# A two-layer encoder: layer 1's attention turned by DMA instead of TensorE, with its steps spread further apart

## The chip, the cores and the metric

The kernel runs on one core of a Trainium2 chip. The metric is the time of one execution on the device, in microseconds (us); the times given are medians of several runs. The core has five engines, each with an instruction queue of its own that it works through strictly in order: TensorE (PE, with PEld for its weight loads), VectorE (DVE), ScalarE (ACT), GpSimd (POOL) and SyncE (SP). Engines wait for one another through semaphores. DMA transfers are issued from the queues of SP, ACT and POOL.

## The reference

The input is 256 tokens of width 2048 and 256 memory tokens. Two layers follow each other. Layer 0 mixes tokens by a gated MLP over chunks, layer 1 by grouped-query attention; both also cross-attend with four heads into the memory, and each is followed by a SwiGLU feed-forward network. The part that the change touches is the attention of layer 1:

```python
def gqa_axial_attention(qkv, g_q, g_k, cos, sin):
    q, k, v = jnp.split(qkv, [TOK_WIDTH, TOK_WIDTH + KV_WIDTH], axis=-1)   # 12 query heads, 4 key heads of 128
    q = apply_axial_rope(rms_norm(q, g_q), cos, sin)
    k = apply_axial_rope(rms_norm(k, g_k), cos, sin)
    ...
        s = jnp.einsum('bqhgd,bkhd->bhgqk', qi, k).astype(jnp.float32) * scale
        p = jax.nn.softmax(s, axis=-1).astype(v.dtype)
        return jnp.einsum('bhgqk,bkhd->bqhgd', p, v)
```

Everything is in float32.

## The kernel before

**Products in three matmuls.** Each float32 operand is split into a rounded half `hi` (ACT, a cast) and the rest `lo` (DVE, a subtraction); `matmul3` (L186 to L188) adds three products of halves. Weights come by SP's DMA into `raw` (4 buffers) and are split by `halves` into `whi` (L270, ACT) and `wlo` (L271, DVE), three buffers each. In layer 1's mixing each split is done in two instructions of 128x1024.

**Linear layers and ticks.** `linear(parts, w, n0)` makes 512 output columns for both token tiles of 128: 96 matmuls of 128x512 into two PSUM banks `acc`. The pool of `acc` has four banks, so a linear layer can begin only when the results of the one before the last have been read out. After every 12 matmuls comes a `tick()`; `later(n, f)` puts work of another kind n ticks ahead, and so decides where it is recorded between the matmuls. A scheduler then sets the final order of every engine's queue, which is fixed when the kernel is built.

**Layer 1's mixing** runs these linear layers one after the other: own keys, own values, three groups of four query heads (c = 0, 1, 2; here the first, second and third group), memory queries, memory keys, memory values, and then the output projection `w_out` (four linear layers). They are called the first to the eighth layer below, w_out apart; the third to the fifth make the query groups, the sixth the memory queries, the seventh the memory keys, the eighth the memory values.

**A group's attention** (`attend`) has four steps, put at ticks by `waits`: `queries_T` turns the rotary-embedded queries (`turning`, L474 to L481, which read `acc`) so that the head dimension lies on the partitions; `scores` multiplies by the turned keys into a PSUM bank `m` and does the softmax (maximum L557 on DVE, a product on POOL L558, exp L562 on ACT, reciprocal L566 and scaling L568 on DVE, head by head); `turn` turns the probabilities; `weigh` multiplies by the values. The pool `m` has four banks too. Nearly all of these tiles come from one pool of 36 (`big`, `MIX_TILES`); the pool `kept` has 16 of its own. A tile whose pool is full waits until an older one has been used for the last time.

**Two ways to turn a tile.** On TensorE: `transpose4` (L192), or the same four matmuls by the identity in `turn` (L585), 128x128 each, into a bank `m`. By DMA: `turned`, in which an engine sorts the float32 words into two planes of 16 bits (L199), the ACT queue issues a DMA transpose (L200), and after some ticks an engine puts the planes together again (L205), here over the source. Layer 0 and the feed-forward networks turn by DMA already; layer 1's own keys, own queries, their probabilities, and its memory keys and queries are turned by TensorE, the probabilities of its memory attention by DMA.

Of the kernel before, what the change touches and what calls it, by code (L numbers as in the profile page):

```python
# [55 lines left out]
def encoder(ctx: ExitStack, tc: tile.TileContext, x, x_t, mem, mem_t, columns, w_in_a, g_v_a, spatial_t, w_in_b,  # L56
# [33 lines left out]
    def misc():  # L90
        if room["banks"] == 2:
            return banks2()[:, 0]
        return room["m"].tile([P, NB], F32, tag="m", name=nm("m"))
# [13 lines left out]
    def later(delay, fn):  # L107
        queue.append((clock[0] + delay, len(queue), fn))
# [68 lines left out]
    def split(src, shape, home=None):  # L177

        hi, lo = [(home or big)(F32R, shape) for _ in range(2)]
        nc.scalar.copy(hi, src)  # L180
        nc.vector.tensor_tensor(lo, src, hi.bitcast(F32), ALU.subtract)
        return hi, lo

    def matmul3(out, a, b, start, stop):

        nc.tensor.matmul(out, lhsT=a[0], rhs=b[0], start=start, stop=False)  # L186
        nc.tensor.matmul(out, lhsT=a[1], rhs=b[0], start=False, stop=False)  # L187
        nc.tensor.matmul(out, lhsT=a[0], rhs=b[1], start=False, stop=stop)  # L188
# [5 lines left out]
    def turned(src, ticks, then, over=False, copy=nc.scalar.copy, home=None):  # L194


        a, b = [(home or big)(F32, [P, 4, P]) for _ in range(2)]
        planes, back = [i.bitcast(U16).rearrange("p c n -> p (c n)") for i in (a, b)]
        copy(planes.rearrange("p (h n) -> p h n", h=2), src.bitcast(U16).rearrange("p (n h) -> p h n", h=2))  # L199
        nc.scalar.dma_start_transpose(back.rearrange("p (c n) -> p c n", n=P), planes)  # L200

        def finish():
            words = src.rearrange("p (c n) -> p c n", c=4) if over else a
            halves = (src.bitcast(U16) if over else planes).rearrange("p (n h) -> p n h", h=2)
            copy(halves, back.rearrange("p (h n) -> p n h", h=2))  # L205
            then(words)

        later(ticks, finish)
# [275 lines left out]
    def queries(acc, r, gain=None):  # L484

        rh = head_squares(acc, r)
        res = []
        for t in range(NT):
            nc.vector.tensor_scalar(rh[:, 4 * t:4 * t + 4], rh[:, 4 * t:4 * t + 4], r[t], None, ALU.mult)
            if gain is None:  # L490
                res.append(turning(acc[t], rope_t["c"][:, t], rope_t["s"][:, t]))
            else:
                qn = big()
                nc.vector.tensor_tensor(v4(qn), v4(acc[t]), gain.unsqueeze(1).to_broadcast([P, 4, P]), ALU.mult)
                res.append(qn)
        return res, rh
# [17 lines left out]
    def heads_T(qn, dma=False):  # L514

        hi = [big(F32R, [P, 2, S]) for _ in range(2)]
        lo = [big(F32R, [P, 2, S]) for _ in range(2)]

        def halves_of(t, whole):
            ts = slice(t * P, (t + 1) * P)  # L520
            for pr in range(2):
                src = whole[:, 2 * pr:2 * pr + 2, :]
                nc.scalar.copy(hi[pr][:, :, ts], src)
                nc.vector.tensor_tensor(lo[pr][:, :, ts], src, hi[pr][:, :, ts].bitcast(F32), ALU.subtract)

        for t in range(NT):
            if dma:
                turned(qn[t], 3, lambda whole, t=t: halves_of(t, whole), True, nc.vector.tensor_copy)
            else:
                tp = misc()  # L530
                transpose4(qn[t], tp)
                halves_of(t, v4(tp))
        return hi, lo

    def attend(qn, waits, keys, values, kv_of, kc0, parts, dma=None, home=None):


        qn, rows = qn
        by_head = rows.rearrange("p (t h) -> p h t", t=NT)
        st = {}  # L540

        def head(p, h):
            return p[0][h // 2][:, h % 2, :], p[1][h // 2][:, h % 2, :]

        def queries_T():
            st["qT"] = heads_T(qn, dma and home is None)

        def scores(pr):
            for h in (2 * pr, 2 * pr + 1):
                kp_ = head(keys(), kv_of(h))  # L550
                qp_ = head(st["qT"], h)
                sc = misc()
                for t in range(NT):
                    ts = slice(t * P, (t + 1) * P)
                    matmul3(sc[:, t * S:(t + 1) * S], (qp_[0][:, ts], qp_[1][:, ts]), kp_, True, True)
                nmx = small(2)
                nc.vector.tensor_reduce(nmx, sc.rearrange("p (t k) -> p t k", t=NT), AX.X, ALU.max, negate=True)  # L557
                nc.gpsimd.tensor_tensor(nmx, nmx, by_head[:, h], ALU.mult)  # L558
                pe = big()
                sm = small(2)  # L560
                for t in range(NT):
                    nc.scalar.activation(pe[:, t * S:(t + 1) * S], sc[:, t * S:(t + 1) * S], AF.Exp,  # L562
                                         bias=nmx[:, t:t + 1], scale=rows[:, 4 * t + h:4 * t + h + 1],
                                         accum_out=sm[:, t:t + 1])
                rcp = small(2)
                nc.vector.reciprocal(rcp, sm)  # L566
                for t in range(NT):
                    nc.vector.tensor_scalar(pe[:, t * S:(t + 1) * S], pe[:, t * S:(t + 1) * S], rcp[:, t:t + 1], None,  # L568
                                            ALU.mult)
                st["p", h] = pe  # L570

        def turn(pr):
            for h in (2 * pr, 2 * pr + 1):
                pn = st["p", h]
                if dma:
                    def halves_of(whole, h=h):
                        hi, lo = split(whole.rearrange("p (t k) n -> p k t n", t=NT), [P, 2, NT, P], home)
                        st["t", h] = [a.rearrange("p k t n -> p (k t n)") for a in (hi, lo)]

                    turned(pn, 3, halves_of, True, nc.vector.tensor_copy, home)  # L580
                    continue
                pt = misc()
                for t in range(NT):
                    for kc in range(2):
                        nc.tensor.transpose(pt[:, kc * S + t * P:kc * S + (t + 1) * P],  # L585
                                            pn[:, t * S + kc * P:t * S + (kc + 1) * P], ident)
                st["t", h] = split(pt, [P, NB])

        def weigh(pr):
            V = values()  # L590
            po = misc()
            for hh in range(2):
                h = 2 * pr + hh
                kv = kv_of(h)
                phi, plo = st["t", h]
                for kc in range(2):
                    vhi, vlo = V[kc]
                    vs, ks = slice(kv * P, (kv + 1) * P), slice(kc * S, (kc + 1) * S)
                    matmul3(po[:, hh * S:(hh + 1) * S], (vhi[:, vs], vlo[:, vs]), (phi[:, ks], plo[:, ks]),
                            kc == 0, kc == 1)  # L600
            hi, lo = split(po.rearrange("p (h s) -> p h s", h=2), [P, 2, S])
            for hh in range(2):
                for t in range(NT):
                    ts = slice(t * P, (t + 1) * P)
                    parts.put(kc0 + 2 * pr + hh, t, hi[:, hh, ts], lo[:, hh, ts])

        later(waits[0], queries_T)
        for wait, f in zip(waits[1:], (scores, turn, weigh)):
            for pr in range(2):
                later(wait + pr, lambda f=f, pr=pr: f(pr))  # L610
# [14 lines left out]
    class Memory:  # L625
# [38 lines left out]

        def attend(self, acc, r, parts, waits, dma, home=None):
            attend(queries(acc, r, ghead[f"mq{self.l}"]), waits, lambda: self.kT, lambda: self.V, lambda h: h, TOK // P,
                   parts, dma, home)

    def add_residual(acc, j, norm, g, parts, dma, copy=nc.scalar.copy):

# [20 lines left out]
    for l in range(DEPTH):  # L691
# [121 lines left out]
                    later(1 + t, lambda u=u, t=t, c=c: turn_u(u, t, c))  # L813
        else:
            w = w_in_b[0]
            own = {}
            load_tables(1)
            m.prep(20, 2)
            acc = linear(hT, w, TOK)
# [7 lines left out]
                    nc.gpsimd.tensor_tensor(s[:, :, h], s[:, :, h], g4[:, :, 1 - h], ALU.mult)  # L827

            def turn_k(kn=kn):
                own["k"] = heads_T(kn)  # L830

            later(7, turn_k)
            own["v"] = scaled(linear(hT, w, TOK + MEMW), norm.r)
            for c in range(3):
                acc = linear(hT, w, c * NB)
                attend(queries(acc, norm.r), (5, 6, 11, 14), lambda: own["k"], lambda: own["v"],
                       lambda h, c=c: (4 * c + h) // 3, 4 * c, cat)
            m.attend(linear(hT, w, TOK + 2 * MEMW), norm.r, cat, (4, 13, 16, 20), True, kept)
            m.keys()
            m.values()  # L840
# [139 lines left out]
```

## Time and profile before

| | |
|---|---|
| median of 3 runs | 1991.22 us (1990.16 to 1991.87) |
| the profiled execution: its time, its span | 1988.33 us, 1986.5 us |
| PE, DVE, ACT, POOL busy | 1975.7, 1645.0, 1217.9, 95.7 us |
| layer 1's mixing in the span | from about 994 to about 1285 us |
| DMA transposes | 78, all from the ACT queue |

A row of the page of groups has the line and engine, the operation, the tiles `out<-in`, the shapes and the count; then busy time and the mean of one, then the engine's idle time before and what ended it. A row of a timeline has the start and the length in us, the engine (ACTq is the issue of a DMA from ACT's queue), the line and the tiles, the count of merged instructions, and in brackets the idle time before the first. Instructions of one engine overlap by a little at their ends, so what one costs in a row of several is the distance from start to start. A row of windows has each engine's busy time, with the count, in one stretch.

### The profile page before, as it was taken

Reading aid. Unit: us, or ns where it says so; the run is one execution under the profiler, and the core shown is the slowest. Engines: PE = TensorE matmul, PEld = TensorE weight load, DVE = VectorE, ACT = ScalarE, POOL = GpSimd, SP = SyncE. Lnnn points to the kernel's source line nnn. Section 1 sums busy time; section 2 is a strip of 40 time slices with the busy share of each in tenths; the row PEclk is TensorE's granted clock in tenths of the full one; section 3 lists DMA queues with packets and bytes.
Section 4 is the critical chain, followed back from the end, with each engine's and each line's share of the span. In section 5 each row is a group of like instructions: output and inputs, shape, how many; then the busy total and the mean of one; then the engine's idle time right before and its main releaser. Section 6 shows DMA issues by size and latency. Waiting matters only on the chain.

```text
span 1986.5 us, 24053 instructions
## 1 busy us (share of the span) xinstructions
PE 1975.7 (99%) x8897; PEld 1636.8 (82%) x8897; DVE 1645.0 (83%) x1755; ACT 1217.9 (61%) x1461; POOL 95.7 (5%) x148
## 2 busy tenths in 40 slices
PE   9999999999999999999999999999999999999998
PEld 7888888888888888888888888888888888888887
DVE  6658778998889989898676866699989889898987
ACT  8756455766546665466766665756665466654673
POOL 2300001000000000000020110010000000000000
PEclk9999999999999999999999999999999999999999
DMA  9867865576775777767866545657767667686674
GB/s 349 300 191 203 242 212 190 189 217 216 231 244 186 220 217 239 235 191 232 239 201 197 168 140 175 217 191 220 226 198 246 212 208 233 195 251 215 202 219 140
DMA packets 287719, 426.99 MB, mean 215 GB/s; under 512 B 93904, under 2 KB 94160, under 8 KB 287600
## 3 DMA queue, kind: packets, MB, share of 16 engines
q1 hardware_dynamic: 199808, 387.62, 58.8%
q10 hardware_dynamic: 82800, 20.91, 6.3%
q0 software_dynamic: 4992, 16.91, 3.8%
q8 instruction: 70, 1.15, 0.2%
q14 instruction: 49, 0.40, 0.1%
HBM read 394.45 MB, written 2.10 MB: 200 GB/s over the span
## 4 chain that ended last, share of the span: by engine, by line
PE 94%; DMA 2%; DVE 2%; ACT 1%; issue 1%; SPq 0%; DVEq 0%; ACTq 0%
PE acc L188 27%; PE acc L186 26%; PE acc L187 26%; PE m L188 5%; PE m L186 5%; PE m L187 5%; DMA a<-a 1%; DVE wlo L271 1%; DMA raw<-in_w_in_a 1%; PE m L192 0%; ACT whi L270 0%; PE m L722 0%; ACT junk L212 0%; PE m L585 0%; DVE T L379 0%
## 5 line engine op out<-in xcount | busy, mean ns | idle before, releaser
L271 DVE TENSOR_TENSOR wlo<-raw,whi 128x2048 fp32r<-128x2048 f32 (+2 forms) x466 | 841.4, 1821 | 202.9 <-ACT whi L270 198.8
L270 ACT CAST whi<-raw 128x2048 fp32r<-128x2048 f32 (+2 forms) x466 | 705.9, 1535 | 434.3 <-PE acc L187 294.5
L186 PE MATMUL acc<-whi,h 128*128 128x512 f32 x1440 | 561.6, 390 | 1.7 <-ACT whi L270 1.7
L187 PE MATMUL acc<-whi,h 128*128 128x512 f32 x1440 | 560.7, 389 | 0.0
L188 PE MATMUL acc<-wlo,h 128*128 128x512 f32 x1440 | 514.8, 390 | 0.1
L186 PE MATMUL acc<-whi,a 128*128 128x512 f32 x999 | 388.3, 390 | 1.0 <-DVE x L457 1.0
L187 PE MATMUL acc<-whi,a 128*128 128x512 f32 x999 | 388.6, 389 | 0.0
L188 PE MATMUL acc<-wlo,a 128*128 128x512 f32 x999 | 365.6, 390 | 0.4 <-DVE wlo L271 0.3
L188 PEld LDWEIGHTS acc<-wlo,h 128*128 128x128 f32 x1440 | 270.3, 188 | 57.9 <-DVE wlo L271 2.0
L186 PEld LDWEIGHTS acc<-whi,h 128*128 128x128 f32 x1440 | 270.4, 188 | 57.4 <-ACT whi L270 2.3
L187 PEld LDWEIGHTS acc<-whi,h 128*128 128x128 f32 x1440 | 270.4, 188 | 55.4
L188 PEld LDWEIGHTS acc<-wlo,a 128*128 128x128 f32 x999 | 187.5, 188 | 40.7 <-DVE wlo L271 2.1
L186 PEld LDWEIGHTS acc<-whi,a 128*128 128x128 f32 x999 | 187.6, 188 | 39.8 <-issue 1.4
L187 PEld LDWEIGHTS acc<-whi,a 128*128 128x128 f32 x999 | 187.6, 188 | 38.8
L270 ACT CAST whi<-T 128x1536 fp32r<-128x1536 f32 x93 | 137.8, 1481 | 119.2 <-PE acc L187 98.7
L271 DVE TENSOR_TENSOR wlo<-T,whi 128x1536 fp32r<-128x1536 f32 x93 | 162.9, 1751 | 4.7 <-PE acc L188 4.7
L379 DVE TENSOR_TENSOR T<-raw 128x1024 f32<-128x1024 f32 x93 | 113.4, 1219 | 19.8 <-DMA raw<-in_w_gate_up 19.7
L186 PE MATMUL m<-whi,a 128*128 128x512 f32 x284 | 110.7, 390 | 0.0
L187 PE MATMUL m<-whi,a 128*128 128x512 f32 x284 | 110.5, 389 | 0.0
L188 PE MATMUL m<-wlo,a 128*128 128x512 f32 x284 | 110.5, 389 | 0.0
L457 DVE TENSOR_TENSOR e<-acc,e 128x512 f32<-128x512 f32 x120 | 79.0, 684 | 1.5 <-PE acc L188 1.3
L205 ACT COPY sg<-a 128x1024 uint16<-128x1024 uint16 x44 | 51.5, 1171 | 30.7 <-DMA a<-a 30.5
(162 smaller groups left out, 1528.0 us busy)
## 6 DMA issues: line engine op xcount, KB each, us to landing
raw<-in_w_gate_up SPq DMA_DIRECT2D x352, 512.0 KB, 4.4
raw<-in_w_down SPq DMA_DIRECT2D x176, 512.0 KB, 5.1
raw<-in_w_out SPq DMA_DIRECT2D x32, 1024.0 KB, 5.3
raw<-in_w_in_a SPq DMA_DIRECT2D x24, 1024.0 KB, 8.0
raw<-in_w_in_b SPq DMA_DIRECT2D x24, 1024.0 KB, 5.1
raw<-in_w_mem_kv SPq DMA_DIRECT2D x16, 1024.0 KB, 5.2
x<-e POOLq DMA_DIRECT2D x16, 512.0 KB, 5.0
a<-in_mem_t POOLq DMA_DIRECT2D x16, 256.0 KB, 5.9
```

The costliest lines, as they stand in the source:

```text
L186: nc.tensor.matmul(out, lhsT=a[0], rhs=b[0], start=start, stop=False)
L187: nc.tensor.matmul(out, lhsT=a[1], rhs=b[0], start=False, stop=False)
L188: nc.tensor.matmul(out, lhsT=a[0], rhs=b[1], start=False, stop=stop)
L205: copy(halves, back.rearrange("p (h n) -> p n h", h=2))
L270: nc.scalar.copy(hi[:, cut], raw[:, cut])
L271: nc.vector.tensor_tensor(lo[:, cut], raw[:, cut], hi[:, cut].bitcast(F32), ALU.subtract)
L379: nc.vector.tensor_tensor(T[:, :2], raw[:, 1:4:2], w01, ALU.add)
L457: nc.vector.tensor_tensor(o[t][n], self.bank[name], o[t][n], op)
```

## The change

Own keys, own queries and all their probabilities are turned by DMA, with DVE doing both copies. That takes away 80 transposes of 128x128 from TensorE and adds 20 DMA transposes and 40 DVE copies of 128x1024 16-bit words. The queries are split per token tile (one cast, one subtraction of 128x512) instead of per head pair. The keys are turned 4 ticks after their layer instead of 7; the steps of the three groups go from ticks 5, 6, 11, 14 to 3, 7, 12, 17. The third group's turned probabilities come from the pool `kept`.

```diff
         def queries_T():
-            st["qT"] = heads_T(qn, dma and home is None)
+            for t in range(NT):
+                if dma_q:
+                    turned(qn[t], 3, lambda whole, t=t: of_tokens(t, whole), True, nc.vector.tensor_copy)
+                else:
+                    tp = misc()
+                    transpose4(qn[t], tp)
+                    of_tokens(t, v4(tp))
...
+        def of_tokens(t, whole):
+            st["q", t] = split(whole, [P, 4, P])
...
-                qp_ = head(st["qT"], h)
                 sc = misc()
                 for t in range(NT):
-                    ts = slice(t * P, (t + 1) * P)
-                    matmul3(sc[:, t * S:(t + 1) * S], (qp_[0][:, ts], qp_[1][:, ts]), kp_, True, True)
+                    qp_ = [a[:, h, :] for a in st["q", t]]
+                    matmul3(sc[:, t * S:(t + 1) * S], qp_, kp_, True, True)
...
             def turn_k(kn=kn):
-                own["k"] = heads_T(kn)
-
-            later(7, turn_k)
+                own["k"] = heads_T(kn, True)
+
+            later(4, turn_k)
...
-                attend(queries(acc, norm.r), (5, 6, 11, 14), lambda: own["k"], lambda: own["v"],
-                       lambda h, c=c: (4 * c + h) // 3, 4 * c, cat)
+                attend(queries(acc, norm.r), (3, 7, 12, 17) if c in (0, 1, 2) else (5, 6, 11, 16), lambda: own["k"],
+                       lambda: own["v"], lambda h, c=c: (4 * c + h) // 3, 4 * c, cat, c in late,
+                       kept if c == 2 else big, c in (0, 1, 2))
```

The order of the queues changes with it, at three places. Numbers in names tell tiles apart, and lines behind L560 are 8 higher in the changed kernel (L557 is L565, L562 is L570 and so on).

The first is PE's queue where the scores of the second group stand. Before (`m_8723` and `m_8741` are two heads' scores, `acc` the linear layer running meanwhile):

```order
L186 MATMUL m_8723<-a_8036,a_8666 128x256
L188 MATMUL acc_8531<-wlo_8762,h_7753 128x512
L186 MATMUL acc_8871<-whi_8875,h_7465 128x512
L187 MATMUL acc_8871<-whi_8875,h_7466 128x512
L187 MATMUL m_8723<-a_8036,a_8668 128x256
L188 MATMUL m_8723<-a_8038,a_8666 128x256
```

They stand between a layer's matmuls, some 100 matmuls behind the group's own linear layer. With the change the scores of the second group (`m_8694`, `m_8712`, `m_8752`, `m_8770`, 24 matmuls) stand behind the last matmul of the sixth layer (`acc_8826`):

```order
L188 MATMUL acc_8826<-wlo_8994,h_7749 128x512
L186 MATMUL m_8694<-a_7980,a_8665 128x256
L186 MATMUL m_8712<-a_7980,a_8665 128x256
L186 MATMUL m_8752<-a_7981,a_8665 128x256
L186 MATMUL m_8770<-a_7981,a_8665 128x256
L187 MATMUL m_8694<-a_7980,a_8666 128x256
```

They are followed by the first group's weighing (`m_8847` and `m_8876`, 24 matmuls), and only then by the first matmul of the seventh layer (`acc_9134`), 48 matmuls of 128x256 in a row with no other work between them:

```order
L186 MATMUL m_8876<-a_8794,a_8070 128x256
L187 MATMUL m_8876<-a_8794,a_8071 128x256
L188 MATMUL m_8876<-a_8795,a_8070 128x256
L186 MATMUL acc_9134<-whi_9138,a_8196 128x512
L187 MATMUL acc_9134<-whi_9138,a_8197 128x512
```

At the end of the seventh layer the same stands once more: 24 scores of the third group, 24 matmuls of the second group's weighing, four transposes of the memory queries, and then the eighth layer.

The second place is DVE's queue, at the softmax of the second group; in brackets the semaphores that an instruction waits for. Before, the turning of the third group's queries, which reads them out of `acc_8530` and `acc_8531`, stands ahead of the fourth head's reciprocal and waits for nothing:

```order
L566 RECIPROCAL s_1457_8810<-s_1456_8807 128x2 [waits Activation_49]
L557 TENSOR_REDUCE s_1459_8821<-m_8814 128x2 [waits PE_49,Pool_49]
L568 TENSOR_SCALAR a_8806<-a_8806,s_1457_8810 128x256 [waits DVE_49]
L568 TENSOR_SCALAR a_8806<-a_8806,s_1457_8810 128x256
L474 TENSOR_TENSOR a_8858<-acc_8530,a_7653 128x512
L479 TENSOR_TENSOR a_8860<-acc_8530,a_7653 128x8x32 x2
L474 TENSOR_TENSOR a_8865<-acc_8531,a_7653 128x512
```

With the change it stands behind the whole softmax and behind the splits of the first group's probabilities (L181), and waits for PE: its output `a_8812` needs a tile of the pool that the first group's weighing (`m_8847`) frees:

```order
L574 RECIPROCAL s_1462_8784<-s_1461_8781 128x2 [waits Activation_49]
L576 TENSOR_SCALAR a_8780<-a_8780,s_1462_8784 128x256 [waits DVE_49]
L576 TENSOR_SCALAR a_8780<-a_8780,s_1462_8784 128x256
L181 TENSOR_TENSOR a_8790<-a_8469,a_8789 128x512 [waits Activation_49]
L181 TENSOR_TENSOR a_8795<-a_8487,a_8794 128x512 [waits PE_49,Activation_49]
L474 TENSOR_TENSOR a_8812<-acc_8522,a_7649 128x512 [waits PE_49]
L479 TENSOR_TENSOR a_8814<-acc_8522,a_7649 128x8x32 [waits PE_49]
```

The seventh layer's `acc_9134` is the bank of `acc_8522`. At the end of the seventh layer the reading of the memory queries (L494, from `acc_8825`) has the same place behind the third group's softmax, and the same wait.

The third place is ACT's queue during the seventh layer. Before, it holds exps, weight splits and casts of the second group there, and no DMA transpose:

```order
L562 ACTIVATE a_9072,s_1510_9073<-m_9062,s_1508_9069,s_1465_8855 128x256 [waits PE_49,Pool_49]
L562 ACTIVATE a_9072,s_1510_9073<-m_9062,s_1508_9069,s_1465_8855 128x256
L180 CAST a_9113<-m_9100 128x512 [waits PE_49]
L270 CAST whi_9359<-raw_9357 128x1024 [waits DMAHW3_49,PE_49]
L270 CAST whi_9359<-raw_9357 128x1024
```

With the change it holds six: the third group's queries (`a_8914`, `a_8918`) and the second group's probabilities:

```order
L200 DMA_TRANSPOSE a_8914<-a_8913 128x8x128 [waits DVE_49]
L200 DMA_TRANSPOSE a_8918<-a_8917 128x8x128 [waits DMAHW2_49,DMAHW1_49,DVE_49]
L270 CAST whi_9302<-raw_9300 128x1024 [waits PE_49]
L270 CAST whi_9302<-raw_9300 128x1024
L200 DMA_TRANSPOSE a_8934<-a_8933 128x8x128 [waits DMAHW2_49,DVE_49]
L200 DMA_TRANSPOSE a_8938<-a_8937 128x8x128 [waits DMAHW3_49,DVE_49]
L270 CAST whi_9383<-raw_9381 128x1024 [waits DMAHW5_49,PE_49]
L270 CAST whi_9383<-raw_9381 128x1024
L200 DMA_TRANSPOSE a_8962<-a_8961 128x8x128 [waits DMAHW4_49,DVE_49]
```

Beside DVE's copy each from the second on waits for a DMA semaphore (DMAHW1 to DMAHW6) that the transpose before it raises when it has landed, so the six go one after the other, with the weight splits behind them in the queue.

More of the change, by code (lines that the diff above doesn't have):

```diff
@@ L533, in heads_T, with attend @@
         return hi, lo
-    def attend(qn, waits, keys, values, kv_of, kc0, parts, dma=None, home=None):
+    def attend(qn, waits, keys, values, kv_of, kc0, parts, dma=None, home=None, dma_q=False):
         qn, rows = qn
@@ L666, in attend @@
             attend(queries(acc, r, ghead[f"mq{self.l}"]), waits, lambda: self.kT, lambda: self.V, lambda h: h, TOK // P,
-                   parts, dma, home)
+                   parts, dma, home, not self.l)
     def add_residual(acc, j, norm, g, parts, dma, copy=nc.scalar.copy):
@@ L815, in encoder @@
             w = w_in_b[0]
-            own = {}
+            own, late = {}, (0, 1, 2)
             load_tables(1)
```

## The prediction, made before the changed kernel ran

> **What bounds the kernel now.** I read the span and the busy times first:
>
> ```profile
> span 1986.5 us, 24053 instructions
> PE 1975.7 (99%) x8897; PEld 1636.8 (82%) x8897; DVE 1645.0 (83%) x1755; ACT 1217.9 (61%) x1461; POOL 95.7 (5%) x148
> ```
>
> PE is busy for 99% of the span. An average can hide a stage with another limit, so next I asked for the chain of waits from 1036 to 1260 us, the stretch with the three groups and the memory attention, and for windows in it (columns: length, PE, PEld, DVE, ACT, POOL, granted clock, DMA share, GB/s):
>
> ```profile
> by line: PE acc L187 28.5%; PE acc L188 28.4%; PE acc L186 28.3%; PE m L187 3.4%; PE m L188 3.4%; PE m L186 3.4%; PE m L192 2.3%; PE m L585 2.3%
> 1050.00:1100.00 50.00, 50.00 (x244) 42.04 (x243) 35.31 (x61) 35.09 (x82) 7.18 (x12) 1.00 0.58 190
> 1100.00:1150.00 50.00, 50.00 (x280) 43.21 (x279) 39.62 (x72) 34.23 (x87) 6.59 (x11) 1.00 0.50 159
> 1150.00:1200.00 50.00, 50.00 (x266) 42.78 (x265) 34.01 (x63) 28.06 (x62) 4.61 (x8) 1.00 0.48 156
> ```
>
> The chain is PE from end to end, and the view of PE's waits has no row here. DVE is busy 34 to 40 us of 50, ACT 28 to 35. So every matmul removed is worth its full length, and every wait that PE is newly given costs its full length: there is no idle time of PE to absorb it.
>
> **What is removed.** 80 transposes by the identity. The chain prices them:
>
> ```profile
> 1036.92 0.44 PE m L192 x4
> 1075.96 0.87 PE m L192 x8
> 1096.11 0.87 PE m L585 x8
> ```
>
> 0.87 us for eight is 0.109 each, 80 of them 8.7 us, all on the path: -8.7. ACT's and DVE's work on their results stays about the same: the queries' splits are only cut otherwise.
>
> **What is added.** 20 DMA transposes on ACT's queue, 40 copies on DVE. Existing ones give the prices (group rows; then the issue line, its landing time, and two issues in the chain):
>
> ```profile
> L199 DVE COPY a<-a 128x1024 uint16<-128x1024 uint16 x14 | 9.4, 686 | 0.1
> L205 DVE COPY a<-a 128x1024 uint16<-128x1024 uint16 x20 | 13.9, 694 | 24.0 <-DMA a<-a 23.9
> L200 ACTq DMA_TRANSPOSE a<-a x74: 1247/1248/3807, 105.8 to 1925.5; - x74
> DMA to landing us min/median/max: 3.0/4.7/9.9
> 1253.46 1.25 ACTq L200 DMA_TRANSPOSE a<-a  x1
> 1259.54 1.25 ACTq L200 DMA_TRANSPOSE a<-a  x1
> ```
>
> 40 copies are 40 x 0.69 = 28 us of DVE and 20 issues 25 us of ACT's queue, spread over some 200 us in which DVE has 10 to 16 us of each 50 free. As throughput that costs nothing. The price lies in who waits for whom, at two places in the order of the queues.
>
> **Place A, the end of the sixth layer.** PE now does 24 scores of the second group and 24 matmuls of the first group's weighing there, with no layer between. The seventh layer needs the bank of `acc_8522`; DVE reads that bank (L474) only after the second group's whole softmax, the splits (L181) and, by the full pool of 36, after the first weighing matmuls on PE. So PE stands until DVE has done all this. Rows of the same operations before:
>
> ```profile
> 1079.39 2.00 ACT L270 CAST whi<-raw 128x1024 fp32r<-128x1024 f32 x2 [0.64 <-PE acc L187]
> 1080.48 2.36 DVE L271 TENSOR_TENSOR wlo<-raw,whi 128x1024 fp32r<-128x1024 f32 x2 [1.15 <-ACT whi L270]
> 1082.76 0.68 DVE L557 TENSOR_REDUCE s<-m 128x2 f32<-128x512 f32 x1
> 1085.14 0.67 DVE L557 TENSOR_REDUCE s<-m 128x2 f32<-128x512 f32 x1
> 1085.72 0.61 DVE L568 TENSOR_SCALAR a<-a,s 128x256 f32<-128x256 f32 x2
> 1087.48 0.69 DVE L557 TENSOR_REDUCE s<-m 128x2 f32<-128x512 f32 x1
> 1094.83 0.68 DVE L474 TENSOR_TENSOR a<-acc,a 128x512 f32<-128x512 f32 x1
> 1095.43 0.75 DVE L479 TENSOR_TENSOR a<-acc,a 128x256 f32<-128x256 f32 x2
> 1096.10 0.47 DVE L243 SCALAR_TENSOR_TENSOR a<-a,cols,a 128x256 fp32r<-128x256 f32 x1
> 1099.59 1.66 POOL L174 TENSOR_TENSOR s<-s,mhalf 128x8 f32<-128x8 f32 x1
> 1095.26 0.39 PE L186 MATMUL acc<-whi,h 128*128 128x512 f32 x1
> 1095.49 0.39 PE L187 MATMUL acc<-whi,h 128*128 128x512 f32 x1
> 1112.07 0.28 PE L186 MATMUL m<-a,a 128*128 128x256 f32 x1
> 1112.19 0.28 PE L187 MATMUL m<-a,a 128*128 128x256 f32 x1
> ```
>
> From start to start, a half of `wlo` is 1.14, a head's softmax 2.36 (its reduction to the next one's: POOL, exp and DVE in turn), L474 0.60, two L479 0.67, a matmul 0.23 at 512 columns and 0.12 at 256. A split (L181) or a copy has the size of L474, so 0.60 in a row of several; the two multiplies of L568 0.53, their 0.61 less the overlap. In order, after the sixth layer's last matmul: a half of the weights that had to wait for it, cast 1.0 and subtracted 1.14 (2.2); four heads (9.4); POOL's power for the memory queries, 1.66, which stands between the heads, nearly hidden once (1.3); then the last two multiplies, two splits, L474 and L479 (0.53 + 1.2 + 0.60 + 0.67 = 3.0). That is 15.9, beside which PE does its 48 x 0.12 = 5.8: 10.1 idle. DVE also comes late. From the first group's scores to here it has 14 halves of `wlo` (16.0), 12 copies (7.3) and some 38 smaller instructions (about 13), 36 us against PE's 189 x 0.23 = 43.5, but six of the copies wait for a transpose, and the last chain of them ends just ahead: I add 2. A = 12.
>
> **Place B, the end of the seventh layer.** Its bunch holds the third group's scores (24), the second group's weighing (24) and four transposes, and the eighth layer then needs the bank that L494 reads behind the third softmax. But those scores need the third group's queries, read only at A, and six DMA transposes (two of queries, four of probabilities) now go one after the other, each waiting on ACT's queue for the landing of the one before, with splits of weights behind it. The last two of them come ahead of the second query split (L181) on DVE. From the seventh layer's start: DVE's rest of the rotation up to the first copy, two L474/L479 sets, two splits and two sums at 0.6, 4.3; six landings at the median, 6 x 4.7 = 28.2, together 32.5; split, copy, two halves of `wlo`, split, 4.1, so 36.6; last scores 0.4; the softmax to its third exp 7.5, there one landing 4.7 more (the third group's own probabilities follow, waited for in the midst of it), and a tail like A's with two more copies, 4.1: 53.3; memory queries' transposes and their bank, 0.6: 53.9. PE's own work in that time is 96 x 0.23 + 5.8 + 0.4 = 28.3. B = 25.6.
>
> The other waits cost nothing: the first group's scores stand where the layer after next is running and its banks have been read, and the keys' transposes have two layers to land. The cover is those layers' 22 us each; without it a landing of 4.7 would show. SP's queue carries weights only; POOL is 5% busy and is moved past nothing but the power priced in A.
>
> **Sum.** 12 + 25.6 - 8.7 = +28.9 us on the profiled execution's 1988.33 us, 1.8 more than its span. The median of the runs shown, 1991.22, is 2.9 above it, so 1991.2 + 28.9 = 2020.
>
> **Bounds.** Landings: at the shortest, 3.0, seven of them take 12 off (2008); at 6.1, the distance of the two chained issues quoted, they add 10 (2030), and DVE's lateness at A could be as long again. The lower bound leaves out all waits for transposes, exps and POOL, and counts DVE's own instructions alone. At A: two halves, four reductions, four reciprocals, eight multiplies, four splits, two small ones and L474 with L479 are 11.0, less 5.8. At B, from the layer's start: eight halves, eighteen copies, eight splits and the same softmax and tail are 33.0, less 28.3. Then 5.2 + 4.7 - 8.7 = +1.2: 1992. I take the median landing, since 4.7 is that of 74 equal transposes under the same load, and nearest to what these meet.
>
> [...] The kernel opens with the same transposes over and over (start:end, length, PE and its count, PEld, granted clock):
>
> ```profile
> 1.35:4.27 2.92, 2.92 (x13) 2.92 (x14) 1.00 0.74 213
> 4.27:5.48 1.21, 1.21 (x13) 1.21 (x11) 1.00 1.05 389
> ```
>
> The first 13 take 2.92 us, the next 13 1.21: about half speed for the first three, though the granted clock reads 1.00. [...]
>
> **Rivals.** *All of it hidden, faster.* The windows leave DVE 10 to 16 us of 50 idle; if it ran so far ahead that the banks were read within PE's 5.8 us at A and 5.8 at B, only the 8.7 would be left: 1991.2 - 8.7 = 1982.5. It decides if DVE reaches L474 within those 5.8 us; against it speaks that 11.0 us of its work there hang on scores that PE makes only at that place. *DVE's work alone.* The transposes land in time beneath the seventh layer, whose 22 us hold four of 4.7; exps overlap the next head's reduction. Then the lower bound holds, 1992, about no change. Against it: the rotation and six landings fill that layer even at the shortest, 4.3 + 6 x 3.0 = 22.3, with splits and softmax still to come. [...] *That the change doesn't do what it says* is excluded by the order: all 20 turns stand in the queues.
>
> **How the numbers follow.** Forecast 0.70, hidden 0.07, DVE's work alone 0.13, slow transposes 0.10. The predicted time is the likeliest's, 2020; its own range is 2008 to 2031. The range given reaches from DVE's work alone to the slow end, 1990 to 2035, which leaves out the hidden case and about half of the slow one, some 0.12, with a little at both edges. A measurement tells about 0.2%, 4 us, from no change: 1987 to 1995. Faster takes the hidden case, 0.07, and a little of the lower bound's; same takes most of the lower bound's, 0.09; slower the rest, 0.83.
>
> **What would show it.** PE's row of transposes L192 and L585 should be shorter by 80 at 0.109. Between the sixth and the seventh layer PE should idle about 12 us, released by DVE's rotation (L474, L479) or the splits ahead of it; between the seventh and eighth about 26, divided between the splits of queries and L494. ACT's queue should hold six transposes in a row, 4 to 6 us apart. The layers ahead of 1080 us and everything behind 1300 should keep their lengths. It would be wrong if DVE had the rotation done early, if landings were near 3, or if the weights' splits behind the transposes on ACT stopped PE inside the seventh layer as well, which the sum counts once only.

## The result, and the profile after

The changed kernel takes 2022.29 us (median of 5 runs, 2016.01 to 2023.3), the kernel before 1990.16 (1988.19 to 1991.87) in the same comparison: ratio 1.0161, 95% interval 1.0147 to 1.0174. It is 32 us slower; 2020 was forecast. The page of the changed kernel has, in the lines that answer to those of before (then TensorE's slices and its granted clock, in tenths):

```profile
span 2020.6 us, 23933 instructions
PE 1982.1 (98%) x8817; PEld 1638.4 (81%) x8817; DVE 1667.8 (83%) x1785; ACT 1218.7 (60%) x1451; POOL 95.3 (5%) x148
PE   9999999999999999999999769999999999999998
PEclk9999999999999999999999879999999999999999
```

80 matmuls are gone, and yet TensorE is busy 6.4 us longer. Its idle time lies in two slices, and there the granted clock falls too. The view of PE's waits between 990 and 1330 us, which had no row before, now says (what waited, on whom, us in total, times, longest):

```profile
PE m L186 <- ACT a L180: 15.9, 6, 6.7
PE m L187 <- DVE a L181: 8.7, 3, 5.1
PE m L188 <- DVE a L181: 2.4, 4, 1.0
```

That is 27.0 us of standing still. L180 and L181 are the two halves of a split, of queries ahead of scores and of probabilities ahead of weighing. Three windows place them: from the end of the sixth layer to the first matmul of the seventh, the seventh, and from its end to the first matmul of the eighth (columns as in the prediction):

```profile
1129.83:1153.04 23.21, 11.42 (x50) 9.98 (x50) 16.13 (x35) 13.73 (x42) 3.53 (x6) 0.67 0.42 130
1153.04:1175.62 22.58, 22.58 (x97) 18.40 (x96) 13.66 (x21) 6.23 (x7) 0.00 (x0) 0.96 0.45 105
1175.62:1203.96 28.34, 13.07 (x54) 11.24 (x53) 21.06 (x41) 14.95 (x44) 3.19 (x6) 0.55 0.60 158
```

The first and third windows hold no layer at all, only the bunches of 48 and 52 matmuls. At 0.12 us a matmul of 256 columns and 0.109 a transpose, as in the kernel before, their work is 5.8 and 6.2 us; the windows last 23.2 and 28.3. A part is idle, and a part is work at a low granted clock: PE is busy 11.4 and 13.1 us with what is worth 5.8 and 6.2. The timeline of PE shows both, in brackets the waits, and in the distance from row to row the speed:

```profile
1129.60 0.39 PE L188 MATMUL acc<-wlo,h 128*128 128x512 f32 x1
1130.42 0.74 PE L186 MATMUL m<-a,a 128*128 128x256 f32 x4 [0.44 <-ACT a L180]
1134.23 0.58 PE L187 MATMUL m<-a,a 128*128 128x256 f32 x1 [3.07 <-DVE a L181]
1138.08 0.28 PE L188 MATMUL m<-a,a 128*128 128x256 f32 x1
1145.04 0.58 PE L186 MATMUL m<-a,a 128*128 128x256 f32 x1 [6.68 <-ACT a L180]
1153.04 0.63 PE L186 MATMUL acc<-whi,a 128*128 128x512 f32 x1
1153.46 0.63 PE L187 MATMUL acc<-whi,a 128*128 128x512 f32 x1
1154.72 0.39 PE L187 MATMUL acc<-whi,a 128*128 128x512 f32 x1
1154.95 0.40 PE L188 MATMUL acc<-wlo,a 128*128 128x512 f32 x1
...
1175.39 0.39 PE L188 MATMUL acc<-wlo,a 128*128 128x512 f32 x1
1177.74 0.74 PE L186 MATMUL m<-a,a 128*128 128x256 f32 x4 [1.97 <-ACT a L180]
1183.55 0.58 PE L187 MATMUL m<-a,a 128*128 128x256 f32 x1 [5.07 <-DVE a L181]
1193.07 0.58 PE L186 MATMUL m<-a,a 128*128 128x256 f32 x1 [3.97 <-ACT a L180]
```

The seventh layer starts at 0.42 us a matmul (1153.04 to 1153.46) and comes back to 0.23 (1154.72 to 1154.95) 1.7 us later. DVE's timeline of the same places tells what PE waited for, first at the end of the sixth layer, then of the seventh:

```profile
1133.48 0.69 DVE L181 TENSOR_TENSOR a<-a,a 128x512 fp32r<-128x512 f32 x1 [1.44 <-DMA a<-a]
1137.62 0.69 DVE L565 TENSOR_REDUCE s<-m 128x2 f32<-128x512 f32 x1 [1.11 <-PE m L188]
1151.20 0.68 DVE L474 TENSOR_TENSOR a<-acc,a 128x512 f32<-128x512 f32 x1
1151.80 0.75 DVE L479 TENSOR_TENSOR a<-acc,a 128x256 f32<-128x256 f32 x2
...
1182.80 0.69 DVE L181 TENSOR_TENSOR a<-a,a 128x512 fp32r<-128x512 f32 x1 [3.78 <-DMA a<-a]
...
1187.92 0.69 DVE L565 TENSOR_REDUCE s<-m 128x2 f32<-128x512 f32 x1 [0.96 <-PE m L188]
...
1202.09 1.28 DVE L494 TENSOR_TENSOR a<-acc,a 128x512 f32<-128x512 f32 x2
```

The second group's queries are split only when their transpose has landed (1133.48), the softmax runs from 1137.62 to 1151, and then only does L474 read the bank that the seventh layer needs. The end of the seventh layer repeats it: split at 1182.80, L494 at 1202.09.

None of PE's waits, though, is put down to L474 or L494. All 27.0 us are put down to the splits (L180, L181), which stand among the same softmaxes in the queues of ACT and DVE. The first bank is read at 1152.55, when L479 ends, and PE, at half speed (0.21 for 0.12), comes to the seventh layer at 1153.04. So in this kernel the late reading is the next wait in line, half a microsecond short of being one, and not the one that PE paid for.

### The profile page after: what moved, and what is told of

The parts are those of the page before. It is cut to its first block, busy times and chain, and to the rows that moved or that the text cites. A ratio compares the mean times of both kernels' runs of the same rounds, so it can differ in the third digit from the quotient of the medians.

```text
span 2020.6 us, 23933 instructions
## 1 busy us (share of the span) xinstructions
PE 1982.1 (98%) x8817; PEld 1638.4 (81%) x8817; DVE 1667.8 (83%) x1785; ACT 1218.7 (60%) x1451; POOL 95.3 (5%) x148
## 5 line engine op out<-in xcount | busy, mean ns | idle before, releaser
L186 PE MATMUL acc<-whi,h 128*128 128x512 f32 x1440 | 560.9, 390 | 1.3 <-ACT whi L270 1.3
L186 PE MATMUL acc<-whi,a 128*128 128x512 f32 x999 | 389.3, 391 | 1.4 <-DVE x L457 1.4
L186 PEld LDWEIGHTS acc<-whi,h 128*128 128x128 f32 x1440 | 270.4, 188 | 57.3 <-ACT whi L270 1.9
L186 PEld LDWEIGHTS acc<-whi,a 128*128 128x128 f32 x999 | 188.1, 188 | 40.5 <-issue 1.8
L186 PE MATMUL m<-whi,a 128*128 128x512 f32 x284 | 110.7, 390 | 0.0
```

## The experiments

Two theories were set against each other, both with the places A and B of the prediction. **Theory 1**: the full pool of 36 tiles makes the splits and the readings of `acc` wait. **Theory 2**: the ticks put the softmax ahead of the reading in DVE's queue, and the pool only adds to it. A rival to both was **load**: 40 copies and 20 issues cost what they cost, wherever they stand. All kernels start from the changed one. The kernel before took 1986.5 to 1987.2 us beside these runs, 3 to 4 less than in the comparison that most forecasts go by, so the ratios are the surer measure. The table has each one's ratio to the kernel before with its interval, PE's waits between 990 and 1330 us in the profile, and the transposes saved at 0.109 us.

| run | turned by DMA | ticks | saved, us | PE waits, us | ratio (95%) |
|---|---|---|---|---|---|
| the change | keys, queries, probabilities | 3, 7, 12, 17 | 8.7 | 27.0 | 1.0161 (1.0147 to 1.0174) |
| q_pe | keys, probabilities | 3, 7, 12, 17 | 6.1 | 15.3 | 1.0086 (1.0070 to 1.0102) |
| p_pe3 | keys, queries | 3, 7, 11, 14 | 3.5 | 7.9 | 1.0057 (1.0041 to 1.0074) |
| raw3 | all, 3 raw buffers | 3, 7, 12, 17 | 8.7 | 24.2 | 1.0492 (1.0473 to 1.0512) |
| raw3mix40 | all, 3 raw buffers, 40 tiles | 3, 7, 12, 17 | 8.7 | 18.5 | 1.0439 (1.0419 to 1.0460) |
| mem4 | all, half the memory | 3, 7, 12, 17 | 8.7 | 20.1 | 1.0091 (1.0074 to 1.0108) |
| w9 | all | 3, 9, 14, 19 | 8.7 | 15.1 | 1.0068 (1.0053 to 1.0083) |
| warm | all, 79 filler matmuls | 3, 7, 12, 17 | 8.7 | 24.5 | 1.0181 (1.0155 to 1.0206) |
| x5 | keys, probabilities | 5, 9, 14, 19 | 6.1 | 15.5 | 1.0057 (1.0045 to 1.0070) |
| x3 | keys, queries, third group's probabilities | 3, 7, 11, 14 (third 17) | 5.2 | 12.1 | 1.0057 (1.0043 to 1.0071) |
| x9 | keys, two groups' queries, third group's probabilities | third 5, 6, 11, 17 | 4.4 | 5.8 | 1.0033 (1.0021 to 1.0044) |
| a_L2 | keys, third group's probabilities | 5, 6, 11, 14 (third 17) | 2.6 | 0 | 0.9995 (0.9986 to 1.0005) |
| y1 | as x9 | third 5, 9, 14, 19 | 4.4 | 0.8 | 0.9981 (0.9972 to 0.9990) |

**q_pe: the queries back to TensorE.**

```diff
-                       kept if c == 2 else big, c in (0, 1, 2))
+                       kept if c == 2 else big, False)
```

> The three groups' queries are turned by TensorE again; keys and probabilities stay with DMA, and the steps stay at ticks 3, 7, 12, 17. Theory (the full pool of tiles makes the queries' splits and the reading of acc late, and PE stands at two places in the queue): six DMA transposes with their 12 tiles leave the pool, no bunch is left at the end of the sixth layer and one of 28 matmuls at the end of the seventh. Place A's 17 us go, place B's 22 shrink to about half, 24 transposes cost 2.6 more: about 1996 us. Rival (the added copies and issues load DVE and ACT, wherever they stand): 12 of 40 copies and 6 of 20 issues go, 30% of the 40 us lost, so 2012 us.

Measured 2003.41 us. Between the sixth and the seventh layer little is left, waits of 0.8, 0.2 and 0.6 us; the rest is at the end of the seventh:

```profile
PE m L186 <- ACT a L180: 12.5, 3, 6.6
PE m L188 <- DVE a L181: 2.2, 3, 1.8
```

So place A comes of the queries' DMA turns, as forecast; whether by their tiles or by their place in the queues, this run does not separate. B did not halve, and the time lies between the two numbers (1996 and 2012): neither theory has its size.

**p_pe3: the probabilities back to TensorE.** `late = ()` and steps at `(3, 7, 11, 14)`.

> The probabilities are turned by TensorE again (steps at ticks 3, 7, 11, 14); keys and queries stay with DMA. Theory: without the probabilities' tiles the pool has room, the reading of acc waits for nothing, no more than 24 matmuls of scores or weighing stand together; 32 transposes fewer than before are worth 3.5 us: 1988 us, at most 1995. Rival (load of the copies and issues): 16 of 40 copies and 8 of 20 issues are left, 40% of 40 us less 3.5: 2003 us.

Measured 1997.76 us, 11.3 more than the kernel before in the same comparison (8.1 to 14.7). Theory 1 had at most 5 more and is missed; load had 12.5 more, which lies within the interval, so this run does not speak against load. Both places are gone in their old form, but a wait has taken their place, in which the third group's turning by TensorE (L593) stands behind the softmax:

```profile
PE m L593 <- ACT junk L466: 3.9, 1, 3.9
PE m L593 <- DVE a L576: 2.1, 1, 2.1
PE acc L186 <- DVE a L494: 1.1, 1, 1.1
```

**raw3 and raw3mix40: room for the pool.** The only space to be had was a buffer of raw weights, so the first is the control of the second.

```diff
-RAW_TILES = 4
+RAW_TILES = 3
-MIX_TILES = 36
+MIX_TILES = 40      # raw3mix40 alone
```

> A control: the changed kernel with three buffers for raw weights instead of four, everything else equal. Weights arrive about 5 us after their issue and a buffer lasts about 5.5 us of matmuls, so three should carry it: 2022 us, up to 2030 if the loads become late in other stages.

> The same control with the space spent on the pool: 40 tiles instead of 36. Theory (pool): the first reading of the third group's acc waits no more for PE, and the bunches shrink from 48 and 52 matmuls to 32 and 28; A from 17 to about 10, B from 22 to about 14: 2005 to 2010 us if the control is at 2022. Rival (the order of DVE's queue and the chain of DMA transposes set both places, the pool doesn't): the reading still stands behind the softmax, less than 4 us are won, 2018 or more.

The control missed: 2084.02 us, since a weight buffer fewer costs waits all over the kernel, of which these two rows of PE's waits (whole span) had 0.3 and 1.7 us before:

```profile
PE acc L188 <- DVE wlo L271: 17.2, 27, 2.0
PE acc L186 <- ACT whi L270: 13.3, 6, 4.0
```

Between the two, 8.4 us are won with four tiles (2084.02 to 2075.66; 10.5 by the ratios, each of which is known to 4 us), and the waits of the stage go from 24.2 to 18.5. That is more than the 4 us of the rival and, by the medians, less than the 12 to 17 of theory 1; the intervals do not exclude 12.

**mem4: the pool's room by leaving out half of the memory.** `prep` loads 4 pairs of tiles instead of 8, and the second 1024 rows of the memory's width are taken from the first's.

```diff
+                self.parts.get = lambda c, t: own(c % 8, t)
...
-            for i in range(8):
+            for i in range(4 if self.l else 8):
```

> The changed kernel with half of layer 1's memory left out (the second 1024 rows of its width are taken from the tiles of the first), which frees 8 of the pool's 36 tiles through the whole stage and takes 8 multiplies of 0.47 us from DVE. The reading of the third group's acc then waits for no tile any more, but still stands behind the second group's softmax. Theory 1 (full pool): A and B go to a third, 1995 to 2000 us. Theory 2 (ticks and queue order): A keeps the softmax, 10 us, B its chain of transposes; 2010 to 2015.

The kernel leaves out half of the memory, so its result is another; its time is what counts here. Measured 2006.54 us, by the ratios 14 us less than the change, between the two theories and nearer to theory 2's 2010. The reading of the third group's `acc` was to wait for no tile here, and PE still waits long at both places, where its longest wait is as long as the change's 6.7:

```profile
PE m L186 <- ACT a L180: 18.5, 6, 6.9
```

So the pool can carry no more than part of the loss, and the places of the splits behind the softmax are enough for waits of their own. How the 14 us divide between the tiles and the 4 us of multiplies left out is not separated.

**w9: other ticks, all turns by DMA.**

```diff
-                attend(queries(acc, norm.r), (3, 7, 12, 17) if ...
+                attend(queries(acc, norm.r), (3, 9, 14, 19),
```

> The changed kernel with one thing else: the groups' steps at ticks 3, 9, 14, 19 instead of 3, 7, 12, 17. Scores are then recorded behind the next group's rotation, which reads acc (a layer is 8 ticks), and the order shows no bunch over 24 matmuls and the rotation ahead of most of the softmax. All 80 transposes stay away from TensorE. Theory 2 (the ticks put the softmax ahead of the reading of acc in DVE's queue; the full pool only adds to it): A goes, of B a few us stay: 1990 us, 1982 if nothing at all is left. Theory 1 (the full pool): the reading still waits for tiles that PE's scores free, so A and B stay at more than half: 2010 or more.

Measured 2001.09 us: of the 32 us lost, 18 come back with three numbers changed, the pool of the same size and all 80 turns still by DMA. How full the pool is from moment to moment changes with the ticks too, and is not shown. Theory 1's bound (2010) is broken, theory 2's number (1990) not reached. Place A is gone; what is left stands at later readings of `acc`, that of the memory values (L627) and of the memory queries (L494), and at the third group's scores:

```profile
PE acc L186 <- DVE a L627: 7.4, 1, 7.4
PE m L186 <- ACT a L180: 4.8, 3, 4.3
PE acc L186 <- DVE a L494: 2.2, 1, 2.2
```

**warm: filler in the idle time.** Matmuls whose results are overwritten, placed in the longest waits.

```diff
+                    for _ in range({4: (20, 0), 8: (36, 0)}.get(kc0, (0, 0))[t] if h == 0 else 0):
+                        nc.tensor.matmul(sc[:, :S], lhsT=qp_[0], rhs=kp_[0], start=True, stop=True)
...
+            for _ in range({0: 14, 4: 9}.get(kc0, 0) if pr == 0 else 0):
+                nc.tensor.matmul(po, lhsT=V[0][0][:, :P], rhs=V[0][0], start=True, stop=True)
```

> The changed kernel with 79 idle-time matmuls whose results are overwritten: 20 and 36 of 128x256 between the first halves of the second and third group's scores (they repeat a score's first matmul), 14 and 9 of 128x512 ahead of the first weighing of the first and second group, into the bank that this weighing starts anew. They fill 2 to 4 us of the four longest waits. Theory (after a wait TensorE runs at half speed for some us, as the rows of 0.43 instead of 0.23 us say, and half of that lies on the path): the matmuls behind the waits go back to 0.12 and 0.23, 6 to 9 us are won: 2013 to 2016. Rival (the slow rows come from elsewhere, the added matmuls run at half speed too): nothing won, up to 5 us lost, 2022 to 2027.

Measured 2023.11 us (2017.27 to 2030.65): nothing won, which is the rival's time. The mechanism is the theory's all the same. The 20 fillers (L564) take 4.43 us, 0.22 each, at a granted clock of 0.50, and the scores behind them come 0.12 apart:

```profile
1138.74 4.63 PE L564 MATMUL m<-a,a 128*128 128x256 f32 x20 [6.76 <-ACT a L180]
1143.17 0.63 PE L186 MATMUL m<-a,a 128*128 128x256 f32 x2
1144.56 0.28 PE L187 MATMUL m<-a,a 128*128 128x256 f32 x1
1144.68 0.28 PE L188 MATMUL m<-a,a 128*128 128x256 f32 x1
1138.74:1143.17 4.43, 4.43 (x21) 0.50 0.29 104
1143.60:1146.48 2.88, 2.88 (x23) 0.96 0.37 142
```

Without filler 14 of the same 24 scores came 0.21 apart (1134.61 to 1137.60 in the change). But these fillers multiply the first half of the queries, so they stood behind the same wait and paid for the slow phase themselves. Fillers from operands that are there earlier were not run. The price of the clock by itself is so not measured.

**a_L2: a small part alone.** `late = (2,)`, no queries by DMA, steps `(5, 6) + ((11, 17) if c in late else (11, 14))`.

> Only the own keys (tick 4) and the third group's probabilities (into the pool kept) are turned by DMA; queries and the other probabilities on TensorE, steps at 5, 6, 11, 14 and, for the third group, 5, 6, 11, 17. 24 transposes fewer than before, 2.6 us; no reading of acc waits for a tile. Theories 1 and 2 alike: no wait is added, 1988 us against 1990.2 of the kernel before. Rival (each added copy on DVE costs, as throughput): 6 DMA transposes and 12 copies of the 20 and 40 cost 0.3 x 40 = 12 us, so 2000.

Measured 1986.02 us against 1987.14: ratio 0.9995, an interval that holds both no change and the 2.6 us saved. PE has no wait at all in the stage, and load's 12 us are excluded.

**x3 and x9: more turns, kept out of the two places.** In both, `late = (2,)`; in x3 all queries by DMA, in x9 those of the first and second group.

```diff
-                       kept if c == 2 else big, c in (0, 1, 2))
+                       kept if c == 2 else big, c in (0, 1))        # x9
```

> Keys, all three groups' queries and the third group's probabilities (into kept) by DMA; the first and second group's probabilities on TensorE. Steps at 3, 7, 11, 14, for the third group 3, 7, 11, 17. 48 transposes fewer than before, 5.2 us; 12 DMA transposes and 24 copies of the change's 20 and 40. In the run with all probabilities on TensorE the waits of PE (8 us) stood at the turning of the third group's probabilities by TensorE; here nothing turns there, and no reading of acc waits for a tile. Theory (waits by place and order, not load): 1986 us and less, against 1988 of the kernel before in the same runs: ratio 0.998. Rival (load of copies and issues): 0.6 x 40 - 5 = 19 us more.

> As the run before it, but the third group's queries on TensorE too, its steps at 5, 6, 11, 17: keys, two groups' queries, the third group's probabilities by DMA. 40 transposes fewer than before, 4.4 us. The third group's queries are then not in a chain of DMA transposes at the end of the stage. Theory: ratio 0.998, 1984 to 1986 us; if the chain of the third group's queries costs the run before it a wait, this one is faster by that wait less 0.9 us. Rival (load): 10 of 20 issues, 0.5 x 40 - 4 = 16 us more.

Both missed on the slow side: 1999.75 and 1994.37 us against 1987.09. Their one large wait is the same, first of x3, then of x9:

```profile
PE m L192 <- DVE a L494: 11.1, 1, 11.1
PE m L192 <- DVE a L494: 3.3, 1, 3.3
```

L494 reads the memory queries' `acc`, and DVE has no idle time in front of it, so no pool holds it up here: it only stands on DVE behind the third group's softmax, all but the end of its fourth head, in a chain with PE, POOL and ACT. In x9 that softmax begins earlier, since no transpose by DMA stands ahead of its scores, and so the reading is 3 us late and not 11. That a reading waits for no tile is so not enough; what stands ahead of it counts as well.

**x5: probabilities by DMA, later ticks.** q_pe's set with `(5, 9, 14, 19)`.

> Keys and all three groups' probabilities by DMA, queries on TensorE, as in the run with the queries put back; but the steps at 5, 9, 14, 19 instead of 3, 7, 12, 17, so that scores are recorded behind the next group's rotation. 56 transposes fewer than before, 6.1 us. Theory 2 (the ticks put reading behind softmax): of the 17 us over the kernel before that the other run lost, at least 12 go: 1985 to 1993 us. Theory 1 (pool): one reading still waits for a tile behind a score on PE, so the loss stays: 2000 us and more.

1999.19 us, 6 better than q_pe by the ratios, where theory 2 had at least 12; the time is nearly theory 1's (2000 and more). The end of the seventh layer is shorter, and the wait has moved on to the third group's weighing and to the next reading:

```profile
PE acc L186 <- DVE a L627: 9.5, 1, 9.5
PE m L188 <- DVE h L181: 4.4, 1, 4.4
```

**y1: x9 with the reading ahead of the softmax.**

```diff
-    (5, 6, 11, 17) if c in late else (3, 7, 11, 14)
+    (5, 9, 14, 19) if c in late else (3, 7, 11, 14)
```

> As the run with keys, two groups' queries and the third group's probabilities by DMA (40 transposes fewer than before, 4.4 us), but the third group's steps at 5, 9, 14, 19 instead of 5, 6, 11, 17. In that run PE waited 3.3 us for L494, which stood on DVE behind three of the third group's four heads. Here the first of its two readings stands ahead of that softmax, the second behind one head and PE's scores of the second. Theory (what costs is an acc reading that stands behind a softmax on DVE): the 3.3 us and their slow clock go, and what is left is the 4.4 us saved less some delays: ratio 0.999 to 1.001, 4 to 8 us faster than that run. Rival (the load on DVE delays the reading wherever it stands): ratio 1.003 as there.

Measured 1983.41 us (1981.89 to 1986.72) against 1987.21: ratio 0.9981 (0.9972 to 0.9990), faster than both kernels and 10 us faster than x9 by the ratios, with the same copies and the same transposes. That is a little better than the 0.999 to 1.001 of the theory and far from the rival's 1.003. DVE's timeline has L494 now ahead of the third group's reductions (the first row) and between the first two (the third):

```profile
1154.91 0.68 DVE L494 TENSOR_TENSOR a<-acc,a 128x512 f32<-128x512 f32 x1
1158.21 0.68 DVE L565 TENSOR_REDUCE s<-m 128x2 f32<-128x512 f32 x1
1159.73 0.69 DVE L494 TENSOR_TENSOR a<-acc,a 128x512 f32<-128x512 f32 x1 [0.84 <-PE m L187]
1161.25 0.67 DVE L565 TENSOR_REDUCE s<-m 128x2 f32<-128x512 f32 x1
```

and PE's waits in the stage have one row left, `PE acc L186 <- DVE a L479` with 0.8 us. 4.4 saved less 0.8 is 3.6; measured are 0.19% of 1987, 3.8 (2.0 to 5.6). With load unchanged and 10 us gone, load is excluded as the cause of x9's loss, and the order is shown to be it. How much of it is the one reading, the two profiles tell in part, whose spans differ by 8.1 us (1990.0 and 1981.9): 3.3 are the wait for it. In the stage x9 also has short waits for splits of weights and activations (0.8, 0.5, 0.4) that y1 has not; that these follow from the reading is not shown, nor how the rest divides.

For the change itself the cause is shown in part: w9 gives 18 of 32 us back by other ticks alone, eight free tiles (with 4 us of multiplies) 14; how far the two overlap stays open, and no run takes the splits, on which PE waited there, out of the softmax by themselves.

## Why the prediction was right

**The removed transposes, -8.7.** Right. The group row of L192 on layer 1's tiles went from 48 to 16 matmuls, and L585's 48 are gone:

```profile
L192 PE MATMUL m<-ident,a 128*128 128x128 f32 x16 | 2.7, 309 | 0.0
```

y1's 3.8 us (2.0 to 5.6) agree with the price: 40 of them are 4.4, less its one wait of 0.8.

**Place A, forecast 12, measured 23.21 - 5.8 = 17.4.** The mechanism was right, the size too small by 5.4. The forecast lets PE stand until the bank is read; the trace puts the waits down to the splits just ahead of that, and the two end within half a microsecond, so the sum holds for either. 3.6 of the 5.4 lie ahead of the softmax: its first reduction came 7.8 us behind the layer's end (1137.62), where the forecast has 4.2. The lateness had been put at 2, but the split of the queries came 3.65 us behind the layer's end (1133.48), and the scores that follow were counted at 0.12 and ran for the most part at 0.21, so that DVE waited 1.1 for them. 1.2 lie between that reduction and L474 (13.6 against 12.4). 0.6 come at the end (1151.20 to 1153.04, 1.8 against 1.3), where the weighing ran at half speed (0.21) up to the seventh layer's first matmul. The clock was left out of the sum.

**Place B, forecast 25.6, measured 22.58 + 28.34 - 28.3 = 22.6.** Too large by 3. Six landings at the median were to take 28.2. The landing times of L200 in two stretches (1150 to 1210, with the six of place B and four of the third group's probabilities, then 1105 to 1130, with six), each with a window from it, say:

```profile
DMA to landing us min/median/max: 3.0/3.1/6.9
1150.00:1160.00 10.00, 9.85 (x40) 8.25 (x41) 7.42 (x16) 1.43 (x3) 0.00 (x0) 0.77 0.14 28
...
DMA to landing us min/median/max: 3.1/5.7/8.6
1110.00:1120.00 10.00, 10.00 (x46) 8.28 (x45) 7.27 (x10) 4.42 (x13) 1.85 (x2) 1.00 1.04 250
```

The transposes of place B began after TensorE had stood still and the weights with it (28 GB/s); four of the six landed in 3.1 us, so that the next was issued as soon after, not 4 to 6 us apart, the other two in 6.3 and 6.9, and the chain from the first issue at 1156.84 to the split at 1182.80 took 26.0. Those ahead of place A met up to 250 GB/s and landed in 5.7 at the median, and the last of them, 5.8, is what the late split waited for. That the traffic makes the difference is likely and not shown by itself: the fifth ahead of A landed in 3.1 in the midst of it. The forecast used one landing, 4.7, for both; it is too long for most of the one and too short for most of the other. It also called 4.7 the median of 74 equal transposes under the same load: it is that of all 78, which stand all over the kernel; the 74 have 5.1, with which the forecast would have come out 3 us higher.

**The sum.** 17.4 + 22.6 - 8.7 = 31.3 of the 34.1 us by which the profiled spans differ; the eighth layer's slow start adds 0.9 (its first four matmuls take 1.85, 1203.96 to 1205.81, at 0.23 they are 0.92), and the rest is spread over the layers outside. The forecast's 28.9 came close in part by luck: A's error, 5.4 too small, and B's, 3.0 too large, go against each other. How much of the 31.3 the clock at half speed makes is not separated.

**The clock.** The upper end of the range, 2035, has 3 us in it for slow starts of TensorE behind the two stalls; no run shows that term. The trace of the change shows a granted clock of 0.50 from 1134.23 to 1137.60, behind a wait of 3.07 us, and from 1145.04 to 1154.32, behind 6.68, where the rows of the program's start had shown 1.00. PE was busy 5.6 and 6.9 us longer in the first and third windows than its work is worth. Not all of that is lost time: DVE's own waits for slow scores are 1.1 (1137.62) and 1.0 us (1187.92).

**The rivals.** Nothing was hidden, so the faster one fell. "DVE's work alone" (1992) fell with the landings in the trace. "Slow transposes", with its 0.10, fell too: the time stayed below 2035, the upper end of the range, and at place B four of six landed in 3.1 us, faster than the median of 4.7; landings ahead of A were longer, 5.7 at the median. The cause named ahead, the full pool, is only part of it: other ticks alone gave back 18 us, eight free tiles 14, and the two intervals overlap.

## What to carry to other kernels

Where TensorE is the bound and accumulators rotate, find in the order of the vector engine's queue what stands ahead of each reading of an accumulator: a softmax there, with its trips to three other engines, made TensorE wait 11.1 us in x3 and 3.3 in x9, though the reading itself waited for nothing. The same holds for the splits that the next matmuls in TensorE's queue need, on which the change itself waited. An operation moved off the bound engine paid here only where these stayed early: 40 of the 80 transposes were worth their 4 us, and all 80 lost 32. In w9 and x5 the waits that were removed reappeared in part at the next such reading, so the whole sequence of readings is to be looked through, not only the two places that a change touches.

## What the runs showed of the hardware

In the traces of the kernel before and of the change, TensorE's waits of up to 1.97 us behind work at full speed left the speed as it was (behind the longest, at 1177.74, four matmuls in 0.74 us at a granted clock of 1.00). Behind 3.07, 6.68 and 5.07 us in the change the matmuls came at about half speed (0.21 for 0.12), and in warm behind 6.76 us too (0.22). In p_pe3 four transposes still ran as fast behind 3.90 us as ahead of it (0.63), and half speed came behind the next wait, of 2.09 us (four transposes in 1.09, then 0.43 for 0.23 a matmul). In two stretches of unbroken work full speed came back after 3.2 us (1134.23 to 1137.4 in the change) and 4.9 us (fillers and scores in warm). Where short waits of 0.15 to 0.84 us interrupted the work it came back later: from 1145.04 on the change was slow for 9.3 us.

A DMA transpose of 128x1024 words of 16 bits landed in 3.1 us where DMA moved 28 GB/s (the two issued between 1150 and 1160), and in 3.1 to 8.6, 5.7 at the median, in the stretch from 1105 to 1130, which has 250 GB/s from 1110 to 1120. One buffer of raw weights (128x2048) fewer cost 66 us by the ratios over the whole kernel, though the landing time of the largest group of weights stayed at its 4.4 us.
